# Order of the high and the low matmuls in the weight-stationary products of a two-layer decoder

## The chip, the cores and the metric

The kernel runs on one core of one Trainium2 chip. The metric is device microseconds of that core for one execution of the whole program, which is one launch. The profile is of one further execution, taken by the hardware profiler. In it PE is TensorE's matmul, PEld its weight load, ACT is ScalarE, DVE is VectorE and SP is SyncE, which issues the DMAs.

## The reference

The computation is a decoder trunk of two layers over 256 tokens of width 2048, in float32: a retention layer, then a block-sparse attention layer, each followed by a squared-ReLU MLP (2048 to 8192 and back) and by a gated per-layer embedding.

```python
proj = xn @ w_in                                  # retention: q, k, v, g
...
h = h + retention(rms_norm(h, ret_norm_g[i]), ret_w_in[i], ret_w_out[i])
...
jnp.square(jax.nn.relu(xn @ w_up)) @ w_down       # MLP
...
gate = jax.nn.sigmoid(rms_norm(h, g) @ w_gate)    # per-layer embedding
return (p_i @ w_up) * gate
...
kv = rms_norm(h, g_kv) @ w_kv                     # shared keys and values
...
q = (xn @ w_q)  ...  out[:, :S] @ w_o             # attention
```

With 256 tokens there is one block of keys, so the attention is causal attention within it. Nearly all the arithmetic is products of a 256-token activation with a large weight matrix.

## The kernel before, in words

**Two-part numbers.** TensorE works here on a float32 format of reduced precision (fp32r). Each float32 operand is therefore split into a high part H and a low part L, H being the value cast to fp32r and L the rest, and a product is computed as H·H + H·L + L·H. A tile of 128 activations by 256 tokens is kept as one tile of 512 columns, H in the first 256 and L in the last 256.

**Weight units.** All weights come as a single stream of 970 units of [128 x 1024] float32. DMAs of SyncE bring two units at a time (1 MB) into a buffer `raw` (three of them). For each unit `conv` makes `wh` on ScalarE (the cast, line 218) and `wl` on VectorE (raw minus wh, line 219), three units ahead of the matmuls (`LOOK = 3`), into four buffers of each kind. The main loop `run` does, for unit i: issue the load for unit i + 6, convert unit i + 3, issue the matmuls of unit i, then whatever tasks were registered for i (evacuations, statistics, the small matmuls of attention and retention). The order on each engine is this program order, with semaphores between the engines.

**Weight-stationary products.** `phase_a` uses them for q and k of the retention's heads 1 to 7, its output projection, both MLP products, the gate, and the attention's k, q and output. A unit is eight blocks of 128 inputs by 128 outputs. For each block k, `mm_a` issues two matmuls into a PSUM bank of 512 columns. The first has `wh` of the block as the stationary operand and all 512 columns of the activation tile (H and L) as the moving one (line 158, "high" below). The second has `wl` as stationary and the 256 columns of H as moving, and adds to the right half of the bank (line 159, "low"). The evacuation adds the two halves. A product of 2048 inputs has two units to a tile, one of 4096 has four. The last tile of each gate product is "narrow": three matmuls of 256 columns for each block, all into one half (lines 154 to 156).

**Other products.** The first head's q and k use `phase_d`, with the same two matmuls in its own loop (lines 189 and 190). v, g and the attention's v use `phase_b`: the activation is stationary and 512 columns of weights move (lines 209 to 211). The per-layer up product has 256-column matmuls with the weights stationary (lines 563 to 565). The retention's scores (line 419) and the attention's logits (line 670 and on) are small matmuls between units.

**A store in the middle.** In the first MLP, `bias_rows` writes 3 MB of position bias rows to DRAM through the same queue as the weight loads (line 613).

Of the kernel before, what the change touches and what calls it, by code (L numbers as in the profile page):

```python
# [17 lines left out]
P = 128  # L18
S = 256
# [20 lines left out]
def order_a(tiles, per, lead):  # L40
    out = [(n, u) for u in range(per) for n in range(lead)]
    return out + [(n, u) for n in range(lead, tiles) for u in range(per)]
# [31 lines left out]
class Core:  # L74
# [3 lines left out]
        self.units, self.tasks = [], {}  # L78
        self.raws, self.ready = {}, {}

# [1 line left out]
    def unit(self, src, j, mm):  # L82
        self.units.append((src, j, mm))
        return len(self.units) - 1
# [37 lines left out]
                fn()  # L122

    def steps(self, i, gen, each=1):
        """the steps of an evacuation: the first after unit i, then each of them per unit"""
        if not next(gen, True):
            self.at(i + 1, lambda: self.more(i + 1, gen, each))

# [15 lines left out]
    def small(self, name):  # L144
        return self.wp.tile([P, S], F32, name=name, tag="small", bufs=6)

# [1 line left out]
    def mm_a(self, ps, wh, wl, rhs, first, last, narrow=False):  # L148
        mm = self.nc.tensor.matmul
        for k in range(8):  # L150
            c = slice(k * P, (k + 1) * P)
            if narrow:
                o, x = ps[:, :S], rhs[k]
                mm(o, wh[:, c], x[:, :S], start=first and k == 0, stop=False)
                mm(o, wh[:, c], x[:, S:], start=False, stop=False)
                mm(o, wl[:, c], x[:, :S], start=False, stop=last and k == 7)
                continue
            mm(ps, wh[:, c], rhs[k], start=first and k == 0, stop=False)  # L158
            mm(ps[:, S:], wl[:, c], rhs[k][:, :S], start=False, stop=last and k == 7)  # L159

    def phase_a(self, name, src, base, tiles, per, lead, rhs, evac, narrow=(), rush=()):
        """tiles of [128 outputs, 256 tokens]; rhs(k) is the (H|L) tile of 128 inputs;
        a narrow tile is summed in one half of its bank"""
        banks, ends = {}, {}
        for j, (n, u) in enumerate(order_a(tiles, per, lead)):
            def mm(wh, wl, n=n, u=u):
                if u == 0:
                    banks[n] = self.bank(f"{name}{n}")
                self.mm_a(banks[n], wh, wl, [rhs(u * 8 + k) for k in range(8)], u == 0, u == per - 1, n in narrow)
            i = self.unit(src, base + j, mm)  # L170
            if u == per - 1:
                ends[n] = i
                self.at(i, lambda n=n, i=i: self.steps(i, evac(n, banks.pop(n)), 4 if n in rush else 2 if n == tiles - 1 else 1))
        return ends

    def phase_d(self, name, src, rhs, evac):
        """4 tiles of [128 outputs, 256 tokens] by units of 4 tiles of inputs and 2 of outputs"""
        banks = {}
        for u in range(4):
            for v in range(2):  # L180
                def mm(wh, wl, u=u, v=v):
                    m = self.nc.tensor.matmul
                    for n in (2 * v, 2 * v + 1):
                        if u == 0:
                            banks[n] = self.bank(f"{name}{n}")
                        ps = banks[n]
                        for j in range(4):
                            c, x = slice((4 * (n % 2) + j) * P, (4 * (n % 2) + j + 1) * P), rhs(4 * u + j)
                            m(ps, wh[:, c], x, start=u + j == 0, stop=False)
                            m(ps[:, S:], wl[:, c], x[:, :S], start=False, stop=u == 3 and j == 3)  # L190
                i = self.unit(src, 2 * u + v, mm)
                if u == 3:
                    for n in (2 * v, 2 * v + 1):
                        self.at(i, lambda n=n, i=i: self.steps(i, evac(n, banks.pop(n))))

    def phase_b(self, name, src, base, rhs, evac):
        """[256 tokens, 512 outputs] as two banks"""
        banks = []
        for u in range(KD // 2):
            def mm(wh, wl, u=u):  # L200
                if u == 0:
                    banks.extend(self.bank(f"{name}{t}") for t in range(2))
                for j in range(2):
                    k = 2 * u + j
                    x, c = rhs(k), slice(j * 512, (j + 1) * 512)
                    for t in range(2):
                        a, b = slice(t * P, (t + 1) * P), slice(S + t * P, S + (t + 1) * P)
                        mm_ = self.nc.tensor.matmul
                        mm_(banks[t], x[:, a], wh[:, c], start=k == 0, stop=False)  # L209
                        mm_(banks[t], x[:, a], wl[:, c], start=False, stop=False)  # L210
                        mm_(banks[t], x[:, b], wh[:, c], start=False, stop=k == KD - 1)  # L211
            i = self.unit(src, base + u, mm)
        self.at(i, lambda: evac(banks))
        return i

# [1 line left out]
    def split(self, dst_h, dst_l, src):  # L217
        self.nc.scalar.copy(dst_h, src)  # L218
        self.nc.vector.tensor_sub(dst_l, src, dst_h.bitcast(F32))  # L219

    def fold(self, dst, ps):
        """dst = the two halves of a bank added"""
        self.nc.scalar.copy(dst, ps[:, :S])  # L223
        self.nc.vector.tensor_add(dst, dst, ps[:, S:])  # L224

    def scaled_h(self, n, g):
        """(h * g) of tile n: the high part of H|L"""
        t = self.slot(f"x{g}_{n}", dt=F32R)
        gs = self.g[:, g, n:n + 1]
        self.nc.scalar.activation(t[:, :S], self.h[n], AF.Copy, scale=gs)  # L230
        return t
# [16 lines left out]
            self.nc.vector.tensor_add(self.acc, self.acc, sq)  # L248

    def rsqrt(self, dst, src, eps, n):  # L250
        """dst = (src + eps) ** -0.5; small tiles"""
        v = self.nc.vector
        a = self.cp.tile([P, n], F32, name="rs_a", tag="rs_a", bufs=2)
        y = self.cp.tile([P, n], F32, name="rs_y", tag="rs_y", bufs=2)
        w = self.cp.tile([P, n], F32, name="rs_w", tag="rs_w", bufs=2)
        v.tensor_scalar_add(a, src, eps)
        v.tensor_single_scalar(y.bitcast(I32), a.bitcast(I32), 1, ALU.logical_shift_right)
        v.tensor_scalar(y.bitcast(I32), y.bitcast(I32), -1, 0x5F3759DF, op0=ALU.mult, op1=ALU.add)
        for c in (3.0, 12.0, 768.0):
            v.tensor_mul(w, y, y)  # L260
            v.tensor_mul(w, w, a)
            v.scalar_tensor_tensor(y, w, c, y, op0=ALU.subtract, op1=ALU.mult)
        v.tensor_scalar_mul(dst, y, -1.0 / 8192.0)
# [22 lines left out]
        self.at(i, self.stats_a)  # L286
        self.at(i + 2, lambda: self.stats_b(**kw))

# [1 line left out]
    def start(self):  # L290
        nc, cp, io = self.nc, self.cp, self.io
        self.ones = cp.tile([P, 2], F32, name="ones")
# [196 lines left out]
        return hi, lo  # L489

    def finish(self, n, gains):
        """tile n of the stream is whole: its scaled splits and its squares"""
        xs = [self.scaled_h(n, g) for g in gains]
        sq = self.square(n)
        yield
        for x, g in zip(xs, gains):
            self.scaled_l(n, g, x)
        self.gather(n, sq)
        self.xx[n] = xs[0]
        if len(xs) > 1:  # L500
            self.x2[n] = xs[1]
# [314 lines left out]
```

## Time and profile before

| | us |
|---|---|
| median of 3 runs | 2832.81 (2832.39 to 2833.46) |
| span of the profiled execution | 2831.3 |
| TensorE matmuls busy in the span | 2798.1 (99%) |
| weight loads busy | 2417.3 (85%) |
| VectorE busy | 1807.1 (64%) |
| ScalarE busy | 1347.6 (48%) |
| DMA: bytes moved | 521.95 MB, mean 184 GB/s |

The profile gives no time for the profiled execution beyond its span; the span leaves out what lies before the first and behind the last instruction, and is 1.5 us below the median of the runs. Matmuls overlap in the records (a matmul's end is modelled, and the next one starts before it), so TensorE's busy share says only that it hardly ever had nothing to do. How fast it works is read from the starts of consecutive matmuls. TensorE's granted clock is full in all but three short stretches: at the start, behind one stall at 1442 us, and at the end.

### The profile page before, as it was taken

How to read it: one execution, taken by the hardware profiler on the slowest of the kernel's cores; microseconds unless marked ns; L12 is line 12 of the kernel's file. 1: busy time of each engine (PE TensorE's matmuls, PEld its weight loads, DVE VectorE, ACT ScalarE, POOL GpSimd, SP SyncE). 2: the span in 40 equal slices, each digit the busy share in tenths (PEclk: the TensorE clock that was granted, in tenths of full speed). 3: DMA queues.
4: the chain of work that ended last, by engine and by line, in shares of the span. 5: the costliest groups of instructions: out<-in, count | busy, mean ns of one | idle time of the engine just before them, and what ended most of it. 6: DMA issues, size and time to landing. Idle time of an engine off the chain costs nothing.

```text
span 2831.3 us, 37950 instructions
## 1 busy us (share of the span) xinstructions
PE 2798.1 (99%) x15482; PEld 2417.3 (85%) x15482; DVE 1807.1 (64%) x2633; ACT 1347.6 (48%) x1901; POOL 0.2 (0%) x4
## 2 busy tenths in 40 slices
PE   9999999999999999999979999999999999999998
PEld 7888888888888888888868888888888888888887
DVE  7766666655566555665647876667665556666566
ACT  5444444444454434444436655555444434444454
POOL 0000000000000000000000000000000000000000
PEclk9999999999999999999989999999999999999998
DMA  6455555555555555555574554545555555555553
GB/s 233 179 181 181 181 182 182 182 199 186 178 194 182 190 184 189 183 189 181 191 185 179 198 181 176 180 170 185 187 184 188 183 189 186 187 190 182 194 182 119
DMA packets 78667, 521.95 MB, mean 184 GB/s; under 512 B 8443, under 2 KB 14492, under 8 KB 16796
## 3 DMA queue, kind: packets, MB, share of 16 engines
q1 hardware_dynamic: 78492, 519.52, 52.1%
q8 instruction: 121, 1.98, 0.3%
q14 instruction: 54, 0.44, 0.0%
HBM read 514.25 MB, written 5.24 MB: 183 GB/s over the span
## 4 chain that ended last, share of the span: by engine, by line
PE 98%; DMA 1%; DVE 0%; ACT 0%; SPq 0%; issue 0%; DVEq 0%; ACTq 0%
PE up L158 17%; PE dn L158 17%; PE up L159 9%; PE dn L159 8%; PE ret_out L158 4%; PE gt L158 4%; PE qk L158 4%; PE ret_out L159 2%; PE ak L158 2%; PE att_o L158 2%; PE aq L158 2%; PE v L209 2%; PE v L211 2%; PE v L210 2%; PE g L209 2%; PE g L211 2%
## 5 line engine op out<-in xcount | busy, mean ns | idle before, releaser
L219 DVE TENSOR_TENSOR wl<-raw,wh 128x1024 fp32r<-128x1024 f32 (+1 forms) x970 | 1180.9, 1221 | 643.9 <-ACT wh L218 633.0
L218 ACT CAST wh<-raw 128x1024 fp32r<-128x1024 f32 (+1 forms) x970 | 1014.6, 1049 | 774.2 <-PE dn L158 277.8
L158 PE MATMUL dn<-a,wh 128*128 128x512 f32 x2048 | 725.2, 399 | 14.5 <-ACT wh L218 14.5
L158 PE MATMUL up<-x,wh 128*128 128x512 f32 x2048 | 724.1, 399 | 0.0
L159 PE MATMUL dn<-a,wl 128*128 128x256 f32 x2048 | 576.1, 281 | 0.5 <-DVE wl L219 0.5
L159 PE MATMUL up<-x,wl 128*128 128x256 f32 x2048 | 575.1, 281 | 0.0
L158 PEld LDWEIGHTS dn<-a,wh 128*128 128x128 f32 x2048 | 385.7, 188 | 111.0 <-ACT wh L218 14.8
L158 PEld LDWEIGHTS up<-x,wh 128*128 128x128 f32 x2048 | 384.8, 188 | 95.8
L159 PEld LDWEIGHTS dn<-a,wl 128*128 128x128 f32 x2048 | 387.9, 189 | 1.0 <-DVE wl L219 1.0
L159 PEld LDWEIGHTS up<-x,wl 128*128 128x128 f32 x2048 | 387.0, 189 | 0.0
L158 PE MATMUL ret_out<-ot,wh 128*128 128x512 f32 x512 | 181.1, 399 | 0.0
L158 PE MATMUL gt<-x,wh 128*128 128x512 f32 x480 | 170.0, 399 | 0.0
L158 PE MATMUL qk<-x,wh 128*128 128x512 f32 x448 | 159.1, 399 | 0.0
L223 ACT COPY t<-up 128x256 f32<-128x256 f32 x128 | 47.6, 372 | 231.7 <-PE up L159 231.7
L159 PE MATMUL ret_out<-ot,wl 128*128 128x256 f32 x512 | 143.8, 281 | 0.0
L159 PE MATMUL gt<-x,wl 128*128 128x256 f32 x480 | 134.7, 281 | 0.0
L224 DVE TENSOR_TENSOR t<-t,up 128x256 f32<-128x256 f32 x128 | 53.9, 421 | 119.9 <-ACT t L223 119.8
L159 PE MATMUL qk<-x,wl 128*128 128x256 f32 x448 | 125.8, 281 | 0.0
L158 PEld LDWEIGHTS ret_out<-ot,wh 128*128 128x128 f32 x512 | 96.2, 188 | 24.0
L158 PEld LDWEIGHTS gt<-x,wh 128*128 128x128 f32 x480 | 90.2, 188 | 22.1
L158 PEld LDWEIGHTS qk<-x,wh 128*128 128x128 f32 x448 | 84.2, 188 | 20.3
L209 PE MATMUL v<-wh,x 128*128 128x512 f32 x256 | 100.5, 392 | 0.0
(311 smaller groups left out, 3459.3 us busy)
## 6 DMA issues: line engine op xcount, KB each, us to landing
raw<-mlp_up SPq DMA_DIRECT2D x128, 1024.0 KB, 4.9
raw<-mlp_dn SPq DMA_DIRECT2D x128, 1024.0 KB, 4.9
raw<-ret_in SPq DMA_DIRECT2D x94, 1024.0 KB, 4.9
raw<-att SPq DMA_DIRECT2D x48, 1024.0 KB, 4.9
raw<-ret_out SPq DMA_DIRECT2D x32, 1024.0 KB, 4.9
raw<-ple_gate SPq DMA_DIRECT2D x32, 1024.0 KB, 4.9
raw<-att_o SPq DMA_DIRECT2D x16, 1024.0 KB, 4.9
raw<-ple_up SPq DMA_DIRECT2D x4, 1024.0 KB, 4.9
```

Of the source, the lines that this page charges most:

```text
L158: mm(ps, wh[:, c], rhs[k], start=first and k == 0, stop=False)
L159: mm(ps[:, S:], wl[:, c], rhs[k][:, :S], start=False, stop=last and k == 7)
L209: mm_(banks[t], x[:, a], wh[:, c], start=k == 0, stop=False)
L210: mm_(banks[t], x[:, a], wl[:, c], start=False, stop=False)
L211: mm_(banks[t], x[:, b], wh[:, c], start=False, stop=k == KD - 1)
L218: self.nc.scalar.copy(dst_h, src)
L219: self.nc.vector.tensor_sub(dst_l, src, dst_h.bitcast(F32))
L223: self.nc.scalar.copy(dst, ps[:, :S])
L224: self.nc.vector.tensor_add(dst, dst, ps[:, S:])
```

## The change

In `mm_a`, outside the narrow case, the two matmuls of a block are no longer issued together. One loop issues the eight high matmuls of the unit, a second one the eight low matmuls. The operands, the destination, the number of matmuls, and the first and last matmul of a bank's sum are the same; the narrow case keeps its order, and `phase_d` and the other products are untouched. Comments and docstrings were also taken out, and lines 158 and 159 of the old kernel are lines 160 and 162 of the new.

```diff
     def mm_a(self, ps, wh, wl, rhs, first, last, narrow=False):
         mm = self.nc.tensor.matmul
-        for k in range(8):
-            c = slice(k * P, (k + 1) * P)
-            if narrow:
-                o, x = ps[:, :S], rhs[k]
+        cut = [slice(k * P, (k + 1) * P) for k in range(8)]
+        if narrow:
+            o = ps[:, :S]
+            for k, c in enumerate(cut):
+                x = rhs[k]
                 mm(o, wh[:, c], x[:, :S], start=first and k == 0, stop=False)
                 mm(o, wh[:, c], x[:, S:], start=False, stop=False)
                 mm(o, wl[:, c], x[:, :S], start=False, stop=last and k == 7)
-                continue
+            return
+        for k, c in enumerate(cut):
             mm(ps, wh[:, c], rhs[k], start=first and k == 0, stop=False)
+        for k, c in enumerate(cut):
             mm(ps[:, S:], wl[:, c], rhs[k][:, :S], start=False, stop=last and k == 7)
```

TensorE's order in the middle of the retention's output projection (`ret_out`; `ot` are the activation tiles, `wh` and `wl` the two parts of a unit). A unit of the kernel before:

```order
L158 MATMUL ret_out_5186<-ot_0_1970,wh_5125 128x512 [waits Activation_49]
L159 MATMUL ret_out_5186<-ot_0_1970,wl_5126 128x256 [waits DVE_49]
L158 MATMUL ret_out_5186<-ot_1_1971,wh_5125 128x512
L159 MATMUL ret_out_5186<-ot_1_1971,wl_5126 128x256
L158 MATMUL ret_out_5186<-ot_2_1972,wh_5125 128x512
L159 MATMUL ret_out_5186<-ot_2_1972,wl_5126 128x256
...
L159 MATMUL ret_out_5186<-ot_3_2547,wl_5126 128x256
L158 MATMUL ret_out_5186<-ot_0_3118,wh_5152 128x512 [waits Activation_49]
L159 MATMUL ret_out_5186<-ot_0_3118,wl_5153 128x256 [waits DVE_49]
```

The same unit of the changed kernel:

```order
L160 MATMUL ret_out_5186<-ot_0_1970,wh_5125 128x512 [waits Activation_49]
L160 MATMUL ret_out_5186<-ot_1_1971,wh_5125 128x512
L160 MATMUL ret_out_5186<-ot_2_1972,wh_5125 128x512
...
L160 MATMUL ret_out_5186<-ot_3_2547,wh_5125 128x512
L162 MATMUL ret_out_5186<-ot_0_1970,wl_5126 128x256 [waits DVE_49]
L162 MATMUL ret_out_5186<-ot_1_1971,wl_5126 128x256
...
L162 MATMUL ret_out_5186<-ot_3_2547,wl_5126 128x256
L160 MATMUL ret_out_5186<-ot_0_3118,wh_5152 128x512 [waits Activation_49]
```

The wait for VectorE's part of the weights moves from the second matmul of the unit to the ninth, and the last matmul that reads `wh` moves from the fifteenth place to the eighth. On ScalarE, which makes `wh`, nothing moves; what its cast waits for (PE_49) is now reached earlier in TensorE's order. Before:

```order
L218 CAST wh_5125<-raw_5031 128x1024 [waits PE_49,Activation_49]
L230 ACTIVATE x_1_5147<-h_87,g 128x256 [waits DVE_49]
L243 ACTIVATE sq_5149<-h_87 128x256
L218 CAST wh_5152<-raw_5073 128x1024 [waits DMAHW4_49,PE_49,Activation_49]
L230 ACTIVATE x_2_5174<-h_87,g 128x256 [waits DVE_49]
```

Changed:

```order
L221 CAST wh_5125<-raw_5031 128x1024 [waits PE_49,Activation_49]
L233 ACTIVATE x_1_5147<-h_87,g 128x256 [waits DVE_49]
L246 ACTIVATE sq_5149<-h_87 128x256
L221 CAST wh_5152<-raw_5073 128x1024 [waits DMAHW4_49,PE_49,Activation_49]
L233 ACTIVATE x_2_5174<-h_87,g 128x256 [waits DVE_49]
```

Only the line numbers differ, by three.

## The prediction

> **What bounds the kernel now.** I read the page first, then the groups of instructions, then the matmuls one by one. The page's head and first part, and four groups of its part 5 and one of the groups kept apart by shape (what follows the bar is busy time, mean length of one, idle time before them):
>
> ```profile
> span 2831.3 us, 37950 instructions
> PE 2798.1 (99%) x15482; PEld 2417.3 (85%) x15482; DVE 1807.1 (64%) x2633; ACT 1347.6 (48%) x1901; POOL 0.2 (0%) x4
> L158 PE MATMUL up<-x,wh 128*128 128x512 f32 x2048 | 724.1, 399 | 0.0
> L159 PE MATMUL up<-x,wl 128*128 128x256 f32 x2048 | 575.1, 281 | 0.0
> L209 PE MATMUL v<-wh,x 128*128 128x512 f32 x256 | 100.5, 392 | 0.0
> L211 PE MATMUL v<-wh,x 128*128 128x512 f32 x256 | 99.8, 390 | 0.0
> L563 PE MATMUL pu<-ph,wh 128*128 128x256 f32 x64 | 18.1, 283 | 0.0
> ```
>
> TensorE is busy in 99% of the span. Only a change in how fast its matmuls follow one another can move the time by much. Lengths overlap, so the price of a matmul is the step from its start to the next start. In the alternating order, in the retention's output projection, across two units (start and length in us):
>
> ```profile
> 599.84 0.40 PE L158 MATMUL ret_out<-ot,wh 128*128 128x512 f32 x1
> 600.07 0.28 PE L159 MATMUL ret_out<-ot,wl 128*128 128x256 f32 x1
> 600.19 0.40 PE L158 MATMUL ret_out<-ot,wh 128*128 128x512 f32 x1
> ...
> 602.67 0.40 PE L158 MATMUL ret_out<-ot,wh 128*128 128x512 f32 x1
> ```
>
> From the first row to the last are eight pairs (each high, 512 columns, then low, 256): 2.83 / 8 = 0.3538 us a pair, the high step about 0.236 and the low about 0.118. What does the same width cost among its own kind? The product of the gate g has only 512-column matmuls, each with another stationary operand:
>
> ```profile
> 68.82 0.39 PE L210 MATMUL g<-wl,x 128*128 128x512 f32 x1
> 69.05 0.39 PE L211 MATMUL g<-wh,x 128*128 128x512 f32 x1
> ...
> 73.81 0.39 PE L211 MATMUL g<-wh,x 128*128 128x512 f32 x1
> ```
>
> From 68.82 to 73.81 lie 22 steps: 4.99 / 22 = 0.2268. The per-layer up product has only 256-column ones, with wh or wl stationary, and the gate product follows it:
>
> ```profile
> 1498.54 0.28 PE L563 MATMUL pu<-ph,wh 128*128 128x256 f32 x1
> 1498.65 0.28 PE L564 MATMUL pu<-pl,wh 128*128 128x256 f32 x1
> ...
> 1509.92 0.28 PE L565 MATMUL pu<-ph,wl 128*128 128x256 f32 x1
> 1510.04 0.40 PE L158 MATMUL gt<-x,wh 128*128 128x512 f32 x1
> 1510.28 0.28 PE L159 MATMUL gt<-x,wl 128*128 128x256 f32 x1
> ...
> 1512.51 0.40 PE L158 MATMUL gt<-x,wh 128*128 128x512 f32 x1
> ```
>
> It has 4 units of 24, so 96 steps from 1498.54 to 1510.04: 11.50 / 96 = 0.1198. Then 1510.04 to 1512.51 are seven alternating pairs: 2.47 / 7 = 0.3529. So a pair costs 0.353 to 0.354 (I take 0.3533) while its two widths, each among their own, cost 0.2268 + 0.1198 = 0.3466. **Alternation costs 0.0067 us a pair.** The lengths in the first fence say the same by another reading: a high matmul in the alternation lasts 399 ns, one in a row of its kind 390 to 392, a low one 281 against 283.
>
> Is this dearness the turn from one width to the other, or the operands (weights stationary here, moving in g)? Where a run of 256-column matmuls ends in an all-512 product:
>
> ```profile
> 1649.71 0.40 PE L209 MATMUL av<-wh,x 128*128 128x512 f32 x1
> 1649.95 0.40 PE L210 MATMUL av<-wl,x 128*128 128x512 f32 x1
> 1650.18 0.39 PE L211 MATMUL av<-wh,x 128*128 128x512 f32 x1
> 1650.41 0.39 PE L209 MATMUL av<-wh,x 128*128 128x512 f32 x1
> ```
>
> The first step is 0.24 and the following ones 0.23, with weights moving and x stationary; the step at 1510.04, with weights stationary, is 0.24 as well. So the first 512 behind a 256 is dear whatever it reads, and the second is not. That carries the forecast. The other turn is cheap (the scores have six 256s behind a 512; two to a row):
>
> ```profile
> 66.97 0.39 PE L211 MATMUL g<-wh,x 128*128 128x512 f32 x1
> 67.20 0.40 PE L419 MATMUL sc<-qh,kh 128*128 128x256 f32 x2
> 67.43 0.40 PE L419 MATMUL sc<-ql,kh 128*128 128x256 f32 x2
> ```
>
> The 512 before a 256 takes 0.23, and two 256s take 0.23: the first of them some 0.11.
>
> **The change part by part.** Nothing is added or removed: 16 matmuls and 16 weight loads a unit, as before. The matmuls of these lines, from the windows view of L158 and then of L159 over the whole span:
>
> ```profile
> 0.00:2831.30 2831.30, 2231.11 (x6304) 1185.44 (x6304) 0.99 0.52 184
> 0.00:2831.30 2831.30, 1770.83 (x6304) 1192.03 (x6304) 0.99 0.52 184
> ```
>
> That is 6304 / 8 = 788 units. A unit now: 8 x 0.3533 = 2.826. A unit changed:
> - the first high, behind a low: 0.236 (rows 0.24, and the alternation's own);
> - seven highs behind a high: 7 x 0.2268 = 1.588;
> - the first low, behind a high: 0.117 (bounds 0.11 from the scores, 0.12);
> - seven lows behind a low: 7 x 0.1198 = 0.839.
>
> Sum 2.780, so 0.047 us less a unit, and 788 x 0.047 = 37 us. The rows have steps of 0.01, which bounds it: with 0.24 for the first high, 0.12 for all lows and 0.3529 a pair, 2.823 - 2.788 = 0.035 and 28 us; with no surcharge at the turns but the first low at 0.11 and 0.3538 a pair, 2.830 - 2.763 = 0.067 would be 53 us, but that denies the 0.24 just quoted; with 0.234 there it is 2.830 - 2.771 = 0.059 and 46 us. I keep 28 and 46 as ends, and 37 as nearest to the rows with many steps.
>
> All eight lows add to the same 256 columns of the bank, one step apart. This costs nothing extra: the up product does so six at a time at 0.1198.
>
> **Waits.** The first high still waits for ScalarE's wh, the first low for VectorE's wl, eight places on. All waits of TensorE for weights in steady work are these, from the view of waits:
>
> ```profile
> PE dn L158 <- ACT wh L218: 14.5, 1, 14.5
> PE dn L159 <- DVE wl L219: 0.5, 1, 0.5
> ```
>
> One each. The cover is long. The conversion runs three units ahead (LOOK). These are the two steps for one unit, begun as the last high matmul of an old unit let go of the buffer:
>
> ```profile
> 600.98 1.05 ACT L218 CAST wh<-raw 128x1024 fp32r<-128x1024 f32 x1 [1.78 <-PE ret_out L158]
> 602.07 1.23 DVE L219 TENSOR_TENSOR wl<-raw,wh 128x1024 fp32r<-128x1024 f32 x1 [1.61 <-ACT wh L218]
> ```
>
> This wl is ready at 603.30 and used by the first low of the unit three on, in the changed order not before 600.9 + 3 x 2.78 + 1.82 = 611.1 (in the old one 600.9 + 3 x 2.83 + 0.24 = 609.6): 6.3 us to spare in the old and 7.8 in the new. For wh, needed at the unit's start, three faster units take 0.14 us of some 7.3 (602.03 to 609.4). The cast waits for the last high matmul of an old unit, now the 8th of 16 and not the 15th, so it is released some 0.9 us sooner (2.47 + 0.40 against 1.60 + 0.39 after the unit's start); nobody is waiting for it, so I cost it at nothing. If this cover were gone, at most VectorE's 1.23 would show in a unit. The evacuation of a bank hangs on its last low, which still ends the unit.
>
> The 14.5 us is one stall, behind a 3 MB store of bias rows:
>
> ```profile
> 1417.29 0.68 SPq L613 DMA_DIRECT2D bvec<-bv  x1
> ...
> 1456.80 0.80 PE L158 MATMUL dn<-a,wh 128*128 128x512 f32 x1 [14.49 <-ACT wh L218]
> 1458.06 0.58 PE L159 MATMUL dn<-a,wl 128*128 128x256 f32 x1 [0.46 <-DVE wl L219]
> 1458.44 0.63 PE L158 MATMUL dn<-a,wh 128*128 128x512 f32 x1
> ...
> 1461.64 0.53 PE L158 MATMUL dn<-a,wh 128*128 128x512 f32 x1
> ```
>
> The weights in hand lasted from the store to 1456.80 - 14.49 = 1442.3, 25 us; at 1.6% less they last 0.4 less, so the stall grows by 0.4. Behind it eight highs now run before the first low, so the 0.46 goes. The five pairs from 1458.44, at half clock, take 3.20 / 5 = 0.640 each; whether a turn costs anything at that clock no row tells, and it is one unit of 788. Together I count nothing, with 2 us either way for where the slow clock begins and ends.
>
> The sum: 2831.3 - 37 = 2794 of span. The profiled span lies 1.5 below the runs' median of 2832.8, so **2795.8 us**; the ends 28 and 46, widened by 2 and rounded, give 2784 to 2807.
>
> **Rivals.**
> *No change (2832.8).* Each matmul has a price by its own width and operands, 0.236 and 0.118 here, and the order of eight and eight is only a permutation. For it: the trace has no 512 behind a 512 with wh stationary. Against it: the step at 1649.71 is dear with the other operands, and the one after it is not. The Trainium skill has such a rule: TensorE: Matmul & The Clock Gate, "Back-to-back issue gap", gives N/2.4 + 2.5 ns for a matmul of N columns and "LDWEIGHTS" 128/1.2 = 107 ns for a load under it, both independent of the neighbour; an estimate by it is 325 ns a pair in either order, so no change, and the trace's 353 disagrees with it.
>
> *Slower (2849).* The highs keep 0.236 because it belongs to weights that ScalarE wrote standing in the array under a 512-wide tile of x, while the lows lose the 0.118 that they have behind a high and take 0.1198 in a run. Place: the first half of each unit. Price: 8 x (0.236 + 0.1198) = 2.846, 0.020 a unit, 16 us. It decides from a high step of 0.3533 - 0.1198 = 0.2335 in a run. The 0.1198 is as good as certain from the up product; the 0.236 has against it what the first rival has, and the up product, with weights that ScalarE wrote standing in the array, shows no surcharge for it.
>
> **How the numbers follow.** Forecast 0.85, no change 0.08, slower 0.07. Some 0.2% (5.7 us) is what a measurement of this kernel tells from no change: all of the forecast's range lies beyond it. Faster 0.85, same 0.08, slower 0.07. The range 2784 to 2807 is the forecast's own and leaves out both rivals, 0.15 together.
>
> **What would show it.** In the changed profile: highs of 512 at 390 to 392 ns in place of 399, lows at 283; seven of eight high steps 0.227, low steps 0.12; a unit of 2.78; no new row of waits for TensorE, and the one stall at 14 to 15. It is wrong if the high steps stay above 0.2335, or if low steps in a run rise: each ns on all lows is 6304 x 0.001 = 6.3 us, so near 0.1265 (0.1198 + 0.047 / 7) the gain is gone. A wait for wl at the ninth matmul of a unit, in more than the stall's unit, would say that the cover was misread.

## The result

The changed kernel takes **2807.11 us** (median of 4 runs, 2805.78 to 2807.53) against 2833.11 (2832.39 to 2833.46) for the kernel before: a ratio of 0.991, 95% interval 0.9896 to 0.9924. It is faster by 26 us. The forecast was 2795.8, 37 us faster, with 2784 to 2807 as its range: the direction held, the size came out at 0.7 of the forecast, a tenth of a microsecond outside the range.

The page of the changed kernel, its head, first part and the groups that answer to those shown before (high matmuls are now line 160, low ones 162, v and the like 212 to 214):

```profile
span 2805.2 us, 37950 instructions
PE 2772.9 (99%) x15482; PEld 2422.7 (86%) x15482; DVE 1803.8 (64%) x2633; ACT 1346.6 (48%) x1901; POOL 0.2 (0%) x4
L160 PE MATMUL dn<-a,wh 128*128 128x512 f32 x2048 | 514.8, 393 | 14.5 <-ACT wh L221 14.5
L160 PE MATMUL up<-x,wh 128*128 128x512 f32 x2048 | 513.2, 392 | 0.0
L162 PE MATMUL up<-x,wl 128*128 128x256 f32 x2048 | 285.5, 282 | 0.0
L213 PE MATMUL v<-wl,x 128*128 128x512 f32 x256 | 99.7, 389 | 0.0
```

TensorE still bounds the kernel at 99%. Nearly all of the 26.1 us of span is in its pace: the high matmuls' mean length fell from 399 to between 392 and 394 ns, most of the way to the 389 of the product v, which has one width, but not all of it. The low ones rose from 281 to 282 or 283. The summed busy time of a group is no price here: overlaps within a run count once, so it fell with the order alone. The starts in the output projection (eight matmuls to a row) give the unit:

```profile
597.57 2.00 PE L160 MATMUL ret_out<-ot,wh 128*128 128x512 f32 x8
599.41 1.12 PE L162 MATMUL ret_out<-ot,wl 128*128 128x256 f32 x8
600.36 0.63 PE L160 MATMUL ret_out<-ot,wh 128*128 128x512 f32 x2
```

Eight highs take 1.84, eight lows 0.95, the unit 2.79 (2.826 before, 2.780 forecast). The first row also tells that the highs are dearer than forecast: its 2.00 is seven steps and the length of the last matmul, 0.39, so seven steps take 1.61, or 0.230 each in place of 0.2268. Taken apart by place in the unit (steps between starts, median over the 788 units, worked out from all starts in the trace; ns):

| matmul of the unit | 1 | 2 | 3 | 4 | 5 | 6 | 7 | 8 |
|---|---|---|---|---|---|---|---|---|
| high | 233 | 236 | 228 | 232 | 231 | 227 | 227 | 227 |
| low | 113 | 119 | 120 | 120 | 120 | 120 | 120 | 120 |

**Five of the eight highs are dear, not one.** TensorE's waits for weights in the changed kernel (before, there were two rows for `dn` and one for the first head):

```profile
PE dn L160 <- ACT wh L221: 14.5, 1, 14.5
PE qk L192 <- ACT wh L221: 2.1, 2, 1.6
```

The second row belongs to the first head, at the start, whose order is untouched (2.6 us before). The single stall is as long as it was, and the 0.5 us for wl behind it is gone. No wait took the place of anything.

### The profile page after: what moved, and what is told of

Its sections match the earlier page's. It is cut to its first block, busy times and chain, and to the rows that moved or that the text cites. A ratio compares the mean times of both kernels' runs of the same rounds, so it can differ in the third digit from the quotient of the medians.

```text
span 2805.2 us, 37950 instructions
## 1 busy us (share of the span) xinstructions
PE 2772.9 (99%) x15482; PEld 2422.7 (86%) x15482; DVE 1803.8 (64%) x2633; ACT 1346.6 (48%) x1901; POOL 0.2 (0%) x4
## 4 chain that ended last, share of the span: by engine, by line
PE 98%; DMA 1%; DVE 0%; ACT 0%; SPq 0%; issue 0%; DVEq 0%; ACTq 0%
PE up L160 17%; PE dn L160 16%; PE up L162 9%; PE dn L162 8%; PE ret_out L160 4%; PE gt L160 4%; PE qk L160 4%; PE ret_out L162 2%; PE ak L160 2%; PE att_o L160 2%; PE aq L160 2%; PE v L212 2%; PE v L213 2%; PE v L214 2%; PE g L212 2%; PE g L214 2%
## 5 line engine op out<-in xcount | busy, mean ns | idle before, releaser
L160 PE MATMUL dn<-a,wh 128*128 128x512 f32 x2048 | 514.8, 393 | 14.5 <-ACT wh L221 14.5
L160 PE MATMUL up<-x,wh 128*128 128x512 f32 x2048 | 513.2, 392 | 0.0
L162 PEld LDWEIGHTS dn<-a,wl 128*128 128x128 f32 x2048 | 280.2, 191 | 20.1
L162 PEld LDWEIGHTS up<-x,wl 128*128 128x128 f32 x2048 | 279.4, 190 | 20.0
L162 PE MATMUL dn<-a,wl 128*128 128x256 f32 x2048 | 286.4, 283 | 0.0
L162 PE MATMUL up<-x,wl 128*128 128x256 f32 x2048 | 285.5, 282 | 0.0
L212 PE MATMUL v<-wh,x 128*128 128x512 f32 x256 | 100.4, 392 | 0.0
L213 PE MATMUL v<-wl,x 128*128 128x512 f32 x256 | 99.7, 389 | 0.0
L212 PE MATMUL g<-wh,x 128*128 128x512 f32 x256 | 99.6, 389 | 0.0
L214 PE MATMUL v<-wh,x 128*128 128x512 f32 x256 | 99.6, 389 | 0.0
L160 PEld LDWEIGHTS gt<-x,wh 128*128 128x128 f32 x480 | 86.3, 189 | 15.4
L213 PE MATMUL g<-wl,x 128*128 128x512 f32 x256 | 99.6, 389 | 0.0
```

## The experiments

All edits are in `mm_a`, on top of the changed kernel. "Surcharge" below is the mean time of a unit above 8 x (0.2268 + 0.1200) = 2.774 us, from the steps between starts in the high and low matmuls, without stalls. It is 52 ns in the kernel before and 21 in the changed one.

**Is it the width, or the two kinds of weights?** The lows were made as wide as the highs, once in turns and once in groups of eight. The edit of the grouped run; in turns, the same two calls stand in one loop:

```diff
-            mm(ps[:, S:], wl[:, c], rhs[k][:, :S], start=False, stop=last and k == 7)
+            mm(ps, wl[:, c], rhs[k], start=False, stop=last and k == 7)
```

> Edit: the low matmul takes all 512 columns of the activation (it adds the product of the two low parts, which the kernel otherwise leaves out), and high and low stand in turns as in the kernel before. All matmuls of a unit are then of one width. Width theory: no step is dear, each 227 (a pair 454), and order makes no difference: about 2807 + 6304 x (0.4536 - 0.3493) = 3464 us, the same as with the groups of eight. Operand theory (what is dear is the change of weights between the two parts, or of the part of the bank that is written): the pair costs 454 + 6.5, and this run is some 26 us above the grouped one.

> Edit: as the run with wide low matmuls in turns, but eight highs first, then eight wide lows. Width theory: 3464 us, within 2 us of the run in turns. Operand theory: some 26 us below that run.

Measured: 3458.0 us in turns and 3458.1 grouped (ratios to the kernel before 1.2209, interval 1.2189 to 1.223, and 1.221, 1.2192 to 1.2228). The groups in turns, then grouped:

```profile
L160 PE MATMUL up<-x,wh 128*128 128x512 f32 x2048 | 797.1, 389 | 0.0
L161 PE MATMUL up<-x,wl 128*128 128x512 f32 x2048 | 796.7, 389 | 0.0
```

```profile
L160 PE MATMUL up<-x,wh 128*128 128x512 f32 x2048 | 506.2, 389 | 0.0
L162 PE MATMUL up<-x,wl 128*128 128x512 f32 x2048 | 505.8, 389 | 0.0
```

All four are at 389 ns, the length in a stream of one width, and the medians differ by 0.1 us where the operand theory wanted 26. So the surcharge arises only where widths change, and does not belong to the change between wh and wl. (Both times lie 6 us under the 3464 forecast, and the stall behind the store is 7 to 8 us shorter: 6.7 and 6.4 us in place of 14.5.) The part of the bank these two runs do not separate from the width, since a wide low also writes the whole bank. The changed trace does: behind the up product, whose 96 matmuls of 256 columns write banks of their own, the highs of the gate product step 233, 236, 229, 232, 231 and then 227, as they do behind lows of their own bank. The prediction's two rivals rested on the operands: a 512-column matmul with weights that ScalarE wrote standing in the array costs 0.227 here like any other.

**Where in the program is it paid?** Odd units issue their lows first, so that two units of a tile make runs of 16. Three theories are put to the test here and in the next two runs: *turn*, each run of highs pays at its start because lows stand before it; *unit*, the highs pay because a new unit with its new weights begins; *debt*, each low leaves a fixed amount that later highs pay in whatever order. The added lines, which replace the two loops (`u` is the unit's number within the tile):

```diff
+        low_first = u % 2 == 1
+        for part in ((1, 0) if low_first else (0, 1)):
+            for k, c in enumerate(cut):
+                end = last and k == 7 and part == (0 if low_first else 1)
+                if part == 0:
+                    mm(ps, wh[:, c], rhs[k], start=first and k == 0, stop=end)
+                else:
+                    mm(ps[:, S:], wl[:, c], rhs[k][:, :S], start=False, stop=end)
```

> Edit: every odd unit of a tile issues its eight lows first and its highs second, so that two units make a run of 16 highs, 16 lows. The places where a 512-column matmul follows a narrower one fall from 873 to 553. Turn: 320 turns less, each 18 to 20 ns net (25 surcharge, less 5 to 7 that the first lows save; the trace shows 25 behind 8 lows and 24.5 behind 104, so 16 lows cost no more): 6 us less, 2801 us, and in the second unit of a tile the highs step 227 from where the run has had five. Unit: as many units begin as before, so 2807. Debt: 16 lows leave twice what 8 leave, so 2807.

Measured: 2801.56 us (2800.8 to 2802.41), ratio 0.9891 (0.9874 to 0.9907): the turn theory's 2801. Where the tiles follow one another in this order:

```profile
700.24 3.82 PE L164 MATMUL ret_out<-ot,wh 128*128 128x512 f32 x16
703.90 2.08 PE L166 MATMUL ret_out<-ot,wl 128*128 128x256 f32 x16
705.81 3.82 PE L164 MATMUL ret_out<-ot,wh 128*128 128x512 f32 x16
```

Sixteen highs take 3.66, two units 5.57, so 2.785 a unit against 2.79. The highs of a run are again 233, 236, 228, 233, 231 and then 227 (medians over its 293 runs of 16 highs behind 16 lows), so 16 lows leave no more behind than 8, and a unit that begins in the middle of a run pays nothing. Unit and debt both fall: each wanted 2807. This is the lowest time of the study, by 1.6 us from that of groups of two below, and it beats both kernels.

**Does the price of a turn depend on the length of the runs?** Shorter groups within a unit; the edit for groups of four (with 2 for each of the three 4s it is that for groups of two).

```diff
-        for k, c in enumerate(cut):
-            mm(ps, wh[:, c], rhs[k], start=first and k == 0, stop=False)
-        for k, c in enumerate(cut):
-            mm(ps[:, S:], wl[:, c], rhs[k][:, :S], start=False, stop=last and k == 7)
+        for b in range(0, 8, 4):
+            for k in range(b, b + 4):
+                mm(ps, wh[:, cut[k]], rhs[k], start=first and k == 0, stop=False)
+            for k in range(b, b + 4):
+                mm(ps[:, S:], wl[:, cut[k]], rhs[k][:, :S], start=False, stop=last and k == 7)
```

> Edit: within a unit, four high matmuls, four low, four high, four low. Three theories of the dear highs (in the changed kernel the first five highs of a unit step 233, 236, 228, 232, 231 ns, then 227). Turn: a run of 512-column matmuls pays behind a run of 256-column ones, wherever that is; then the second four highs of a unit are as dear as the first four, and a unit pays two turns. The price of a turn behind four lows lies between the rows for three lows (14 to 18 ns of surcharge, less 7 that the first lows save) and what four highs can pay of the pattern (21, less 7): 7 to 14 net, so 14 to 28 a unit against 20 now, and 2802 to 2813 us. Unit: the first highs of a unit are dear because a new pair of weight buffers begins there, with its waits; then the second four highs step 227, and the time is 2803 to 2807. Debt: each low leaves 3 ns to be paid by later highs, in whatever order; then the surcharge of a unit stays at 25 and the time at 2807.

> Edit: within a unit, two highs, two lows, four times over. Turn: four turns a unit; the price of one lies between that of the alternation (6.5 ns net) and that behind three lows (7 to 11 net): 26 to 44 ns a unit against 20 now and 52 in the alternation: 2812 to 2826 us, with all four pairs of highs alike. Unit: the last six highs step 227, time 2803 to 2807. Debt: 2807, the surcharge 25 in a unit.

Measured: groups of four 2818.11 us (ratio 0.995, 0.9935 to 0.9965), groups of two 2803.21 (0.9897, 0.9882 to 0.9912). The first lies above every number on record, the second below what the turn theory gave; it is in the unit theory's range, but not with its steps, as will be seen. A unit of groups of four, and the start of the next:

```profile
600.90 1.09 PE L161 MATMUL ret_out<-ot,wh 128*128 128x512 f32 x4
601.83 0.63 PE L163 MATMUL ret_out<-ot,wl 128*128 128x256 f32 x4
602.30 1.09 PE L161 MATMUL ret_out<-ot,wh 128*128 128x512 f32 x4
603.23 0.64 PE L163 MATMUL ret_out<-ot,wl 128*128 128x256 f32 x4
603.70 1.09 PE L161 MATMUL ret_out<-ot,wh 128*128 128x512 f32 x4
```

Both groups of highs take 0.93, 0.2325 each, so the second in a unit is as dear as the first: again the turn and not the unit's beginning. But the price of a turn was wrong. In groups of two:

```profile
600.06 0.63 PE L161 MATMUL ret_out<-ot,wh 128*128 128x512 f32 x2
600.52 0.40 PE L163 MATMUL ret_out<-ot,wl 128*128 128x256 f32 x2
600.75 0.63 PE L161 MATMUL ret_out<-ot,wh 128*128 128x512 f32 x2
601.22 0.39 PE L163 MATMUL ret_out<-ot,wl 128*128 128x256 f32 x2
601.45 0.62 PE L161 MATMUL ret_out<-ot,wh 128*128 128x512 f32 x2
```

Two highs and two lows take 0.695 here (600.06 to 601.45 is two groups) and 0.6973 as a mean over all units, 3.7 ns above 2 x 0.3468, where a turn of the alternation costs 6.5. The unit theory wanted the last six highs at 227; by place the steps are 233, 231, 113, 119, then 233, 236, 116, 113, twice over in a unit, so all four groups of highs are dear, and the lows give back most of it. Neighbouring groups differ, in a cycle of eight matmuls. What a group pays depends on the group before it, so more than the last neighbour is remembered.

**One low between highs, and groups of three.** Two runs for that memory, with the order in a unit given as a list (that of the second run is H3 L3 H3 L3 H2 L2); the added lines, in place of the two loops:

```diff
+        at = {"H": 0, "L": 0}
+        for part, n in (('H', 4), ('L', 1), ('H', 4), ('L', 7)):
+            for _ in range(n):
+                k = at[part]
+                at[part] += 1
+                if part == "H":
+                    mm(ps, wh[:, cut[k]], rhs[k], start=first and k == 0, stop=False)
+                else:
+                    mm(ps[:, S:], wl[:, cut[k]], rhs[k][:, :S], start=False, stop=last and k == 7)
```

> Edit: within a unit four highs, one low, four highs, seven lows. The lows behind the first four highs are one in place of four. The first four highs, behind seven lows, should step 233, 236, 228, 232 (21 ns over 227) and the first lows of a run save 5 to 7. What do four highs behind a single low pay? Price by the last low alone, as in the alternation: 236, then 227: 9 ns, a unit 18 over turn-free steps, 2806 us. Memory, a single low interrupts nothing: the recovery goes on as 231, 227, 227, 227: 4 ns, a unit 13 to 15, 2802 to 2804 us. Restart, any low starts the recovery anew: 21 ns, a unit 30, 2815 us.

> Edit: within a unit three highs, three lows, three highs, three lows, two highs, two lows. Groups of one cost 52 ns a unit over turn-free steps, of two 16, of four 35, of eight 20 (from the steps in the traces). If the price goes smoothly between two and four: 25 ns a unit, 2811 us. If it hangs on what earlier runs left behind (memory), no size tells the next one's price and the time may lie outside 2803 to 2818, and the two groups of three in a unit will not show the same steps.

Measured: H4 L1 H4 L7 2804.04 us (ratio 0.9898, 0.9881 to 0.9914), a surcharge of 16 ns; groups of three 2810.35 (0.9921, 0.9906 to 0.9936), 25 ns. A unit of the first:

```profile
601.57 1.09 PE L165 MATMUL ret_out<-ot,wh 128*128 128x512 f32 x4
602.49 0.28 PE L167 MATMUL ret_out<-ot,wl 128*128 128x256 f32 x1
602.61 1.08 PE L165 MATMUL ret_out<-ot,wh 128*128 128x512 f32 x4
603.53 0.98 PE L167 MATMUL ret_out<-ot,wl 128*128 128x256 f32 x7
604.35 1.09 PE L165 MATMUL ret_out<-ot,wh 128*128 128x512 f32 x4
```

The time is at the edge of the memory case (2802 to 2804), but its steps are not: the four highs behind the single low are 231, 224, 231, 236 and not 231, 227, 227, 227, and the seven lows behind them are cheaper than was assumed (116, 113, 117, 118, 119, 121, 117). So the time agrees by a sum of two errors, and this run confirms no theory; it only excludes the restart (2815). Groups of three came out at the smooth case's 2811, with two groups of three that show nearly the same steps (233, 235, 228 and 235, 234, 227).

All orders together, the even ones sorted by the length of a run:

| order in a unit | time, us | turns into 512 a unit | surcharge a unit, ns | a turn, ns |
|---|---|---|---|---|
| 1 and 1 (before) | 2833.1 | 8 | 52 | 6.5 |
| 2 and 2 | 2803.2 | 4 | 15 | 3.7 |
| 3, 3, 2 | 2810.4 | 3 | 25 | 8.3 |
| 4 and 4 | 2818.1 | 2 | 34 | 17 |
| 8 and 8 (changed) | 2807.1 | 1 | 21 | 21 |
| 16 and 16 (partly) | 2801.6 | 0.59 | 13 | 23 |
| H4 L1 H4 L7 | 2804.0 | 2 | 16 | 8 |

In groups of two and more, a turn gets dearer with the length of the run, and little dearer from eight on. What a unit pays is that price times the number of turns: four is the worst of the grouped orders, two and sixteen are the best. The 0.59 of the row for sixteen is 1 less the 320 turns saved, over 788 units.

**Where turns cost nothing.** The trace of the kernel before limits the reading by turns. In 47 of its 788 units the alternation has as many turns as elsewhere and no surcharge. Behind the stretch at half clock:

```profile
1462.48 0.39 PE L158 MATMUL dn<-a,wh 128*128 128x512 f32 x1
1462.71 0.28 PE L159 MATMUL dn<-a,wl 128*128 128x256 f32 x1
1462.83 0.39 PE L158 MATMUL dn<-a,wh 128*128 128x512 f32 x1
...
1498.54 0.28 PE L563 MATMUL pu<-ph,wh 128*128 128x256 f32 x1
```

From the first row to the last are 13 units, 104 pairs: 36.06 / 104 = 0.3467 us a pair, which is the sum of the two widths in streams of their own. The 47 units come in stretches of 1 to 13 that begin at the end of the slow clock or behind small matmuls of another product, and each lasts until other matmuls come between. The other 740 units (the stall's aside) hold 0.353 to 0.354, also from one such interruption to the next. So the alternation has two paces and keeps the one that it began with: a turn of width is needed for the surcharge, but does not bring it about alone. If all units held the cheap pace, 740 x 8 x 0.0066 = 39 us would be saved, more than any order here did; that is an estimate, and how to enter that pace was not tried. Nor does the length of the run ahead fix the price: in the same trace, nine 512-column steps behind three matmuls of 256 columns cost between 14 and 46 ns over 9 x 0.2268, at eight places of the product `av`.

**What stays open.** Why a turn costs something, what TensorE remembers over five to eight matmuls, and what chooses between the two paces, no run settles. In the changed trace the steps depend on the place in the run and hardly on what VectorE does at the time: the second high takes 235.4 ns as a mean with the conversion to wl running through the whole step (39 cases) and 235.3 without it (351), and at the third to the fifth the two differ by at most 0.6 ns. That speaks against a contention with the conversion. The rest is a description by run lengths, not a mechanism.

## Why the prediction was right, and where it was wrong

**Right: what bounds, and that alternation is dear** (in all but those 47 units). The lengths forecast for the changed profile were 390 to 392 for the highs and 283 for the lows; 392 to 394 and 282 to 283 came, so the highs lie a little above. The waits are as forecast: one stall of 14.5, no wait for wl at the ninth matmul. The cover of the conversions was read rightly.

**Wrong: "seven highs behind a high: 7 x 0.2268 = 1.588".** That term was mis-sized. The seven steps are 1.607 us (means over the 786 units without a stall or half clock): the second to the fifth high are dear by 9, 2, 5 and 4 ns, only the last three cost 0.2268. This is 0.0196 us a unit and 15.4 us in 788 units. The other three terms were right or erred by less: the first high is 0.236 as forecast, the first low 0.1134 for 0.117, the seven lows 0.839 as forecast. A unit is so 2.796 in place of 2.780, and 788 x (2.826 - 2.796) = 24 us is what is left of the 37. By the starts in the two traces 24.4 us came from the high and low matmuls of `mm_a`. Of the rest of the 26.1, 1.4 came from the first head's q and k, which the change does not touch; they lie about the slow clock at the start, which I do not count as a gain of the order. That part of the gain is luck.

The step that led there was "the first 512 behind a 256 is dear whatever it reads, and the second is not". It rested on one place, with three 256s ahead, read in steps of 0.01 us; a step of 0.234 shows there as 0.23 and so does one of 0.227. In the nanoseconds of the trace the steps at 1649.71 are 235, 234 and then 227, so the second was dear as well, and at 1656.19, behind the same three 256s, nine steps in a row are dear, by 46 ns in all. The trace of before had the answer at a better place, where the alternation of a head's q and k ends in the product v of one width:

```profile
104.57 0.28 PE L159 MATMUL qk<-x,wl 128*128 128x256 f32 x1
104.68 0.39 PE L209 MATMUL v<-wh,x 128*128 128x512 f32 x1
...
106.77 0.39 PE L209 MATMUL v<-wh,x 128*128 128x512 f32 x1
```

Nine steps lie between 104.68 and 106.77: 2.09 / 9 = 0.2322 by these rows, 0.2313 by the nanoseconds of the trace, and not 0.2268. The 512-column matmuls behind a turn are dear for a whole run of steps, 41 ns in all here and 58 or 59 in the six later heads, and to sum the steps to the ninth would have told it in spite of the rounding. The low end of the range fell with it: 28 us was "0.24 for the first high and 0.12 for all lows", a bound on the rounding of known terms, and it left the same seven highs at 0.2268.

**The rivals.** "No change" needed a price by width and operands alone; the runs with wide lows show that a change of operands costs nothing, and the result that order matters. "Slower" needed highs that stay above 0.2335 in a run; the first two do (0.236 each as a mean), but the mean of eight is 0.2304, about half of the way there from 0.2268.

**The rule by columns.** The formula of the Trainium skill that was weighed (TensorE: Matmul & The Clock Gate, "Back-to-back issue gap"; there for the isolated gap of one matmul) has a price by the columns alone, by which a pair is estimated at 325 ns in any order. A pair took 353.3, 351.1, 349.9, 349.5 and 348.7 ns in the orders of one, four, three, eight and two (means over the same units of each order), so the measurement decides against it: the order matters, and each order is dearer than the formula.

## What to carry to other kernels

When a stream of matmuls bounds a kernel, price each matmul by the step between starts among its own neighbours, and look for turns between widths: a stream that takes 512 and 256 columns by turns lost 52 ns in 2.8 us here, one of a single width nothing. The number of turns does not tell the cost by itself, so try two or three orders (here 2 and 2 or 16 and 16 beat 8 and 8, and 4 and 4 was worst of the groups), and look in the trace for stretches where the same order runs at another pace. To price a turn from a trace, sum eight or more steps behind it: a view that rounds to 0.01 us hides seven nanoseconds that repeat thousands of times.

## What the runs showed of the hardware

- At half clock no constant on top of the columns shows. Behind the stall of the changed kernel, from the windows view (clock 0.50 in the third column from the right) and the timeline:

```profile
1447.30:1448.90 1.60, 1.60 (x9) 1.60 (x8) 0.92 (x1) 1.60 (x3) 0.00 (x0) 0.50 0.23 56
```

```profile
1447.29 1.91 PE L162 MATMUL dn<-a,wl 128*128 128x256 f32 x8
1448.99 2.12 PE L160 MATMUL dn<-a,wh 128*128 128x512 f32 x8
```

Eight lows take 1.70 us, 0.2125 each, and an alternating pair of the kernel before took 0.640 as a mean of five: 768 columns in 0.640 are 1.2 columns a nanosecond, and 256 at that pace 0.2133, which the 0.2125 is within the rounding of the rows. At the full clock (1.00 in the windows view) twice that pace would give 106.7 and 213.3 ns, an estimate, where the steps in streams of one width are 120.0 and 226.7: 13.3 ns on top, the same for both widths. So neither that constant nor the price of a turn shows in these few matmuls at half clock; why, no run tells.
- In the changed kernel and in that with runs of 16, the surcharge on five 512-column matmuls behind a run of 256-column ones is 26 or 27 ns after 8, 16 or 104 of them (the last in two places only), with the same five steps to within 1 ns.
- In the kernel before, the same alternation of 512 and 256 columns at full clock ran at 0.3467 us a pair in 47 units and at 0.353 to 0.354 in 740, and kept to one pace from one interruption to the next.
